# Separate memory for the output projection's split activations, and FNet channel sums over even and odd columns

## The chip, the cores and the metric

One core of a Trainium2 chip runs one layer of a hybrid encoder in float32. The metric is the time of one launch on the device in microseconds, here the median of three runs: 1719.39 (1713.63, 1719.39, 1721.88). The engines are named as in the profile: PE multiplies matrices (PEld are its weight loads), DVE, ACT and POOL do the elementwise work, SP issues most transfers. [...]

## The reference

`x` has 512 positions of 2048 channels. One input projection yields the inputs of four groups of 1024 channels and a gate; each group is normalised, gated, and all are projected back.

```python
h = rms_norm(x, pre_g)
a, f, hy, q, gate = split(h @ w_in)
y_a = silu(layer_norm(depthwise_conv(glu(a)))) @ conv_pw_w + conv_pw_b     # group 0
y_b = fft2(f, axes=(1, 2), norm="ortho").real @ fnet_w + fnet_b            # group 1, FNet
y_c = hyena(hy)                                                            # group 2
y_m = cross_attention(q, mem)                                              # group 3
y = rms_norm_per_group([y_a, y_b, y_c, y_m]) * silu(gate)
return x + rms_norm(y @ w_out, post_g)
```

The change touches three places: the Fourier sums of FNet along its 1024 channels (and the weights after them), the sums of squares of group 0, and the start of the output projection `y @ w_out`.

## The kernel before, in words

All large products are made of three float32r matmuls: each operand is split into a high part (ACT copies it with rounding) and a low part (DVE subtracts), `split`, lines 77 to 83; `mm3` (L111) multiplies high by high, then low by high and high by low in the two cross terms. Since both ACT and DVE make the parts of every weight tile that comes from DRAM (`wload`: a load on SP into one of three `raw` buffers, then `wsplit` into one of three pairs `wh`, `wl`), L79 and L80 are the lines of nearly all their records, and one goes by tiles.

`project` (L313) makes 128 channels of the input projection: two weight tiles of 1024 columns, 24 matmuls of 512 columns under each, so 48 in all. `gate` (L649) is such a projection with a SiLU and a product; `conv_proj` is two of them. `fill` is a generator that is advanced after each 12 matmuls of a projection, so that other work stands between them in the program.

The order of the work: memory keys and values, Hyena filters, Hyena convolutions, FNet (from L661), attention, layer norm and pointwise convolution of group 0 (from L939), the output projection (from L1003). Within this order each engine's own queue is laid out by the framework's planner before the run: at each moment of its estimate an engine takes, of the instructions whose inputs and buffers are there, the one that stands earliest in the program. In the run each engine keeps that order and waits where the estimate was wrong. A tile's buffer is taken from a pool; a tile that comes to lie where a closed pool was waits for that pool's last users.

FNet. The input stage (L678) leaves, for 512 channels, even and odd combinations along the positions in `eeH`/`eeL` (five chunks of 128 channels, the fifth a special row) and `ooH`/`ooL` (four). The channel sums multiply them by cosine and sine tables of 512 columns: three banks `psT` (42 matmuls, one table of 128 x 512 loaded per chunk), a bank `psX` of two-column sums (30 matmuls), two banks `psS` (24 matmuls), lines 728 to 751. After `conv_proj(4)` these banks are split into `teH`, `teL`, `toH`, `toL`, which the sums along the positions read after two more gates (L774). `out_product` (L791) multiplies by `fnet_w` in two halves of four steps, as the filler of `conv_proj(5)` and a gate; in its first step row 0 of `we` is copied by ACT, and one row is loaded into `rx`.

Group 0. With `mean` (L948) DVE subtracts it from eight tiles, ACT squares each and POOL adds the squares to `vacc` (`group_square`, L480); `layer_norm` then sums `vacc` over the channels on PE (L158), ACT and DVE make the reciprocal root, and PE spreads it (L153). It stands in the filler of gate(3, 5), after 36 of its 48 matmuls. The pointwise product's squares are added to `gacc` in the same way (L986). Group 0's last gate follows, then its norm, and 15 DVE operations on its tiles (L500, L998).

The output projection runs in rounds over 512 output columns and in each over 32 pairs of a weight tile and a split activation `jh`, `jl` (L1059); its pool `wp4` is opened where the pool `wp5` of group 0 was closed:

```python
    w5.close()
    w4 = ctx.enter_context(ExitStack())
    wp = w4.enter_context(tc.tile_pool(name="wp4", bufs=3))
    order = [CT * g + ct for g in (2, 1, 3, 0) for ct in range(CT)]
                jh = wt("jh", dt=F32R, bufs=3)
                split(jh[:, c0:c1], jl[:, c0:c1], ys[k // CT][k % CT // 4][:, k % 4, c0:c1])
```

Group 2 comes first in `order`; group 0, the last to be finished, comes last.

Of the kernel before, what the change touches and what calls it, by code (L numbers as in the profile page):

```python
# [20 lines left out]
P = 128  # L21
# [4 lines left out]
KD = D // P  # L26
# [10 lines left out]
C1 = 6.28125  # L37
C2 = 0.0019353071795864769
C3 = 2.0 * math.pi - C1 - float(np.float32(C2))


@with_exitstack
def encoder_kernel(ctx: ExitStack, tc: tile.TileContext, a: dict, out: bass.AP):
# [681 lines left out]
    act.activation(cgxH, cgx[:, 0:10], AF.Copy)  # L725

    NS = ((0, 128), (128, 256), (130, 258))
    psT = [pg() for _ in range(3)]
    psX = pg()
    for c in range(5):  # L730
        raw = load(a["cg"][c], 512)
        th, tl = wsplit(raw[:, 0:512])
        for n in range(3):
            s = slice(*NS[n])
            if c < 4:
                mm3(psT[n], eeH[:, c, s], eeL[:, c, s], th, tl, c == 0, False)
            else:
                pe.matmul(psT[n], eeH[:, c, s], th, start=False, stop=False)
                pe.matmul(psT[n], eeL[:, c, s], th, start=False, stop=True)
    for n in range(3):  # L740
        s = slice(*NS[n])
        for c in range(5):
            pe.matmul(psX[:, 2 * n:2 * n + 2], eeH[:, c, s], cgxH[:, 2 * c:2 * c + 2], start=(c == 0), stop=False)
            pe.matmul(psX[:, 2 * n:2 * n + 2], eeL[:, c, s], cgxH[:, 2 * c:2 * c + 2], start=False, stop=(c == 4))
    psS = [pg() for _ in range(2)]
    for c in range(4):
        raw = load(a["sg"][c], 512)
        th, tl = wsplit(raw[:, 0:512])
        for n in range(2):
            s = slice(P * n, P * n + P)  # L750
            mm3(psS[n], ooH[:, c, s], ooL[:, c, s], th, tl, c == 0, c == 3)
    conv_proj(4, ubm)
    teH = wpo.tile([P, 3, 514], F32R, tag="eeH", name="teH")
    teL = wpo.tile([P, 3, 514], F32R, tag="eeL", name="teL")
    for n in range(3):
        split(teH[:, n, 0:512], teL[:, n, 0:512], psT[n])
        split(teH[:, n, 512:514], teL[:, n, 512:514], psX[:, 2 * n:2 * n + 2])
    toH = wpo.tile([P, 2, 512], F32R, tag="ooH", name="toH")
    toL = wpo.tile([P, 2, 512], F32R, tag="ooL", name="toL")
    for n in range(2):  # L760
# [30 lines left out]
    def out_product():  # L791
        for hf in range(2):
            psE = [pg() for _ in range(4)]
            psO = [pg() for _ in range(2)]
            for k in range(4):
                raw = load(a["fw"][hf, k])
                we, wo = web[:, k % 2, :], wob[:, k % 2, :]
                dve.tensor_tensor(we, raw[:, 512:1024], raw[:, 0:512], op=add)
                dve.tensor_tensor(wo, raw[:, 0:512], raw[:, 512:1024], op=sub)
                if k == 0:  # L800
                    act.activation(we[0:1, :], raw[0:1, 0:512], AF.Copy)
                    rx = stg.tile([P, 1024], F32, tag="raw", name=nm("rx"))
                    dve.memset(rx[:, 0:512], 0.0)
                    sp.dma_start(rx[127:128, 0:512], a["fw"][hf, 0][0:1, 512:1024])
                    xh, xl = wsplit(rx[:, 0:512])
                    for m in range(4):
                        s = slice(P * m, P * m + P)
                        mm3(psE[m][:, 0:258], xh[:, s], xl[:, s], fabH[:, 4, :], fabL[:, 4, :], True, False)
                weH, weL = wsplit(we)
                woH, woL = wsplit(wo)  # L810
                for m in range(4):
                    s = slice(P * m, P * m + P)
                    mm3(psE[m][:, 0:258], weH[:, s], weL[:, s], fabH[:, k, :], fabL[:, k, :], False, k == 3)
                    mm3(psO[m // 2][:, 256 * (m % 2):256 * (m % 2) + 256], woH[:, s], woL[:, s], fobH[:, k, :], fobL[:, k, :], k == 0 and m % 2 == 0, k == 3 and m % 2 == 1)
# [12 lines left out]
            yield  # L827
# [108 lines left out]
    w3.close()  # L936


    w5 = ctx.enter_context(ExitStack())  # L939
    wp = w5.enter_context(tc.tile_pool(name="wp5", bufs=1))  # L940
    lnt = wt("lnt", (P, 4, 512), bufs=1)
    uH = wt("uH", (P, CT, 512), F32R, 1)
    uL = wt("uL", (P, CT, 512), F32R, 1)
    mean = lnt[:, 0, :]
    rstd = lnt[:, 1, :]
    pm = pg()
    pe.matmul(pm, ones, csum, start=True, stop=True)
    act.activation(mean, pm, AF.Copy, scale=1.0 / G)  # L948
# [1 line left out]
    for ct in range(CT):  # L950
        y = acch[ct // 4][:, ct % 4, :]
        dve.tensor_tensor(y, y, mean, op=sub)
        group_square(y, vacc, lnt[:, 2 + ct % 2, :], ct == 0)
    gate(3, 4, yM)

    def layer_norm():
# [16 lines left out]
    for hf in range(2):  # L973
# [8 lines left out]
        for m in range(4):  # L982
            y = yA[hf][:, m, :]
            ct = 4 * hf + m
            act.activation(y, accs[m], AF.Identity, bias=pw_b[:, ct:ct + 1])
            group_square(y, gacc, lnt[:, 2 + ct % 2, :], ct == 0)  # L986
    gA = wt("uL", (P, CT, 512), F32, 1)
    for ct in range(EARLY):
        sp.dma_start(gA[:, ct, :], gdm[:, ct, :])
# [38 lines left out]
    for r, ms in rounds:  # L1028
# [5 lines left out]
        for kp in range(16):  # L1034
# [12 lines left out]
            for kk in range(2):  # L1047
# [8 lines left out]
                    held.append((n, jh, jl, wh, wl))  # L1056
                    continue
                wh, wl = wh2[:, 512 * kk:512 * kk + 512], wl2[:, 512 * kk:512 * kk + 512]
                jh = wt("jh", dt=F32R, bufs=3)  # L1059
                jl = wt("jl", dt=F32R, bufs=3)  # L1060
                split(jh[:, c0:c1], jl[:, c0:c1], ys[k // CT][k % CT // 4][:, k % 4, c0:c1])
                for m in ms:
                    s = slice(P * m, P * m + P)
# [13 lines left out]
def _tables():  # L1077
# [10 lines left out]
    c = np.arange(512)
    ang = 2.0 * np.pi * (np.outer(c, c) % 1024) / 1024.0
    alt = np.tile((-1.0) ** c / P, (P, 1))  # L1090
    t["cg"] = np.concatenate([np.cos(ang).reshape(4, P, 512), alt[None]])
    t["sg"] = np.sin(ang).reshape(4, P, 512)
# [24 lines left out]
def _arrange(inp):  # L1117
# [79 lines left out]
```

## Time and profile before

| | |
|---|---|
| median of three runs | 1719.39 us |
| profiled execution, whole | 1716.29 us |
| its span, first to last instruction | 1714.5 us |
| PE busy | 1655.3 us, 97% of the span |
| DVE busy | 1221.9 us, 71% |
| ACT busy | 813.6 us, 47% |
| POOL busy | 189.9 us, 11% |
| mean granted clock of TensorE | 0.987 |

The page gives shares over the whole span; what a place is worth is read from its own stretch. In a timeline a row is the start, the length, the engine, the line, the operation, what it writes and reads, the shape, and a count; a bracket tells how long the engine had been idle before and whose result ended the wait. Matmuls are pipelined: a row's length is longer than the step to the next row, and it is the step that counts. Steps are taken here between the starts of the first and the last of a number of rows.

### The profile page before, as it was taken

Reading aid. Unit: us, or ns where it says so; the run is one execution under the profiler, and the core shown is the slowest. Engines: PE = TensorE matmul, PEld = TensorE weight load, DVE = VectorE, ACT = ScalarE, POOL = GpSimd, SP = SyncE. Lnnn points to the kernel's source line nnn. Section 1 sums busy time; section 2 is a strip of 40 time slices with the busy share of each in tenths; the row PEclk is TensorE's granted clock in tenths of the full one; section 3 lists DMA queues with packets and bytes.
Section 4 is the critical chain, followed back from the end, with each engine's and each line's share of the span. In section 5 each row is a group of like instructions: output and inputs, shape, how many; then the busy total and the mean of one; then the engine's idle time right before and its main releaser. Section 6 shows DMA issues by size and latency. Waiting matters only on the chain.

```text
span 1714.5 us, 21887 instructions
## 1 busy us (share of the span) xinstructions
PE 1655.3 (97%) x8201; PEld 1386.6 (81%) x8201; DVE 1221.9 (71%) x1835; ACT 813.6 (47%) x1185; POOL 189.9 (11%) x146
## 2 busy tenths in 40 slices
PE   7999999999999999999999999999999699999997
PEld 5997888887777778878888888888878588888876
DVE  7866987378797887989874979985562545454586
ACT  6645655344343443424344355445454434444564
POOL 5101422011020120100000020100212000000000
PEclk9999999999999999999999999999999899999999
DMA  8654545768576684623434334232123523222355
GB/s 290 227 185 156 160 139 158 218 155 176 136 171 150 146 181 126 137 93 106 134 105 133 105 124 153 81 111 86 62 98 109 193 98 102 93 101 98 128 203 179
DMA packets 87487, 240.27 MB, mean 140 GB/s; under 512 B 8915, under 2 KB 26579, under 8 KB 86869
## 3 DMA queue, kind: packets, MB, share of 16 engines
q1 hardware_dynamic: 80468, 213.70, 38.6%
q0 software_dynamic: 6912, 25.17, 7.9%
q8 instruction: 64, 1.05, 0.2%
q14 instruction: 43, 0.34, 0.1%
HBM read 220.21 MB, written 18.63 MB: 139 GB/s over the span
## 4 chain that ended last, share of the span: by engine, by line
PE 78%; DVE 14%; DMA 2%; issue 2%; ACT 2%; POOL 1%; SPq 0%; DVEq 0%; ACTq 0%; POOLq 0%
PE pf L114 14%; PE pf L112 14%; PE pf L113 14%; PE pg L113 11%; PE pg L112 11%; PE pg L114 11%; DVE y L525 5%; DVE wl L80 2%; DVE yc L629 1%; DMA raw<-in_wv_dram 1%; POOL vacc L485 1%; ACT wh L79 1%; DMA wl<-in_w_std_dram 1%; DVE y L630 1%; DVE pq L568 1%
## 5 line engine op out<-in xcount | busy, mean ns | idle before, releaser
L112 PE MATMUL pf<-hH,wh 128*128 128x512 f32 x1280 | 505.6, 395 | 0.0
L114 PE MATMUL pf<-hH,wl 128*128 128x512 f32 x1280 | 502.7, 393 | 0.3 <-DMA wl<-in_w_std_dram 0.3
L113 PE MATMUL pf<-hL,wh 128*128 128x512 f32 x1280 | 502.1, 392 | 0.0
L80 DVE TENSOR_TENSOR wl<-raw,wh 128x1024 fp32r<-128x1024 f32 (+1 forms) x240 | 304.0, 1269 | 151.6 <-ACT wh L79 151.0
L79 ACT ACTIVATE wh<-raw 128x1024 fp32r<-128x1024 f32 (+1 forms) x240 | 247.5, 1033 | 231.3 <-PE pf L113 140.8
L114 PEld LDWEIGHTS pf<-hH,wl 128*128 128x128 f32 x1280 | 241.5, 189 | 49.6 <-DMA wl<-in_w_std_dram 0.7
L113 PEld LDWEIGHTS pf<-hL,wh 128*128 128x128 f32 x1280 | 241.9, 189 | 46.9 <-issue 0.2
L112 PEld LDWEIGHTS pf<-hH,wh 128*128 128x128 f32 x1280 | 241.7, 189 | 46.9 <-issue 0.5
L80 DVE TENSOR_TENSOR jl<-y,jh 128x512 fp32r<-128x512 f32 (+1 forms) x154 | 91.3, 597 | 121.6 <-ACT jh L79 120.5
L79 ACT ACTIVATE jh<-y 128x512 fp32r<-128x512 f32 (+1 forms) x154 | 84.4, 550 | 178.6 <-PE pg L113 113.4
L112 PE MATMUL pg<-wh,jh 128*128 128x512 f32 x384 | 150.6, 392 | 11.2 <-ACT jh L79 11.2
L113 PE MATMUL pg<-wl,jh 128*128 128x512 f32 x384 | 150.5, 392 | 0.0
L114 PE MATMUL pg<-wh,jl 128*128 128x512 f32 x384 | 150.4, 392 | 0.0
L107 ACT ACTIVATE wh<-raw 128x1024 fp32r<-128x1024 f32 x48 | 51.0, 1061 | 99.8 <-PE pf L113 51.8
L525 DVE SCALAR_TENSOR_TENSOR y<-ubuf,par,y 128x512 f32<-128x512 f32 x120 | 93.0, 775 | 3.5 <-ACT y L523 1.5
L112 PEld LDWEIGHTS pg<-wh,jh 128*128 128x128 f32 x384 | 72.8, 189 | 26.6 <-ACT jh L79 11.5
L114 PEld LDWEIGHTS pg<-wh,jl 128*128 128x128 f32 x384 | 72.6, 189 | 15.2 <-DVE jl L80 0.2
L113 PEld LDWEIGHTS pg<-wl,jh 128*128 128x128 f32 x384 | 72.7, 189 | 15.1
L108 POOL DMA_DIRECT2D wl<-in_w_std_dram x48 | 41.7, 870 | 286.2 <-ACT wl L106 274.3
L106 ACT ACTIVATE wl<-raw 128x1024 fp32r<-128x1024 f32 x48 | 50.2, 1046 | 0.0
L525 DVE SCALAR_TENSOR_TENSOR y<-ub,par,y 128x512 f32<-128x512 f32 x60 | 46.4, 773 | 2.3 <-ACT y L523 1.1
L1016 POOL TENSOR_TENSOR xres<-xres,og 128x512 f32<-128x512 f32 x4 | 6.7, 1682 | 372.2 <-ACT og L1015 372.2
(380 smaller groups left out, 2916.8 us busy)
## 6 DMA issues: line engine op xcount, KB each, us to landing
raw<-in_w_std_dram SPq DMA_DIRECT2D x160, 512.0 KB, 4.2
raw<-in_wo_dram SPq DMA_DIRECT2D x77, 512.0 KB, 3.3
wl<-in_w_std_dram POOLq DMA_DIRECT2D x48, 512.0 KB, 7.8
raw<-in_wk_dram SPq DMA_DIRECT2D x16, 512.0 KB, 4.0
kd<-y SPq DMA_DIRECT2D x16, 512.0 KB, 4.9
y<-kd SPq DMA_DIRECT2D x32, 256.0 KB, 6.0
raw<-in_w_f_dram SPq DMA_DIRECT2D x16, 512.0 KB, 3.2
raw<-in_wv_dram SPq DMA_DIRECT2D x15, 512.0 KB, 5.2
```

Source lines behind the costliest of these rows:

```text
L79: act.activation(h, src, AF.Copy)
L80: dve.tensor_tensor(l, src, h, op=sub)
L106: act.activation(l, raw, AF.Copy, scale=-1.0)
L107: act.activation(h, raw, AF.Copy)
L108: pool.dma_start(l, src, accum_op=add)
L112: pe.matmul(ps, wh, xh, start=start, stop=False)
L113: pe.matmul(ps, wh, xl, start=False, stop=False)
L114: pe.matmul(ps, wl, xh, start=False, stop=stop)
L485: pool.tensor_tensor(acc, sqt, acc, op=add)
L525: dve.scalar_tensor_tensor(o, u[:, t:t + L], conv_w[:, ct, t:t + 1], o, op0=mul, op1=add)
L568: dve.tensor_tensor(pq[:, 0], z0, z1, op=add)
L629: dve.scalar_tensor_tensor(yv, pcv[:, h], cinv[:, o, ct:ct + 1], yv, op0=mul, op1=add)
```

## The change

In FNet, the 512 channels and their tables are reordered to even ones first, then odd ones (`FNC`). For half of the output frequencies the even and the odd channels are summed apart, into the two halves of a bank, so each table chunk has 256 columns; `both` then forms even plus odd and even minus odd. The cosine table is loaded as one tile of 1024 columns and one of 256, the sine table as one of 1024. The two-column sums go over three chunks instead of five. The rows of `fnet_w` are ordered to match: row 0 of `we` now comes by a transfer at k = 0, a copy of a row is made at k = 2, and `rx` takes a whole row of 1024 and one more add.

`jh` and `jl` get a pool `wj` of two buffers that is opened before group 0's pool; round 0 uses it alone, later rounds use it for two of three tiles and one buffer in `wp4` for the third. To make room, the four tiles `lnt` become one `stat`; in the layer norm ACT squares into a PSUM bank, and DVE instead of POOL adds the squares, there and after the pointwise product.

```diff
+    cgH, cgL = wload(a["cg"][:, 0:1024])
+    raw = load(a["cg"][:, 1024:1280], 256)
+    caH, caL = wsplit(raw[:, 0:256], 256)
-    for c in range(5):
-        raw = load(a["cg"][c], 512)
-        th, tl = wsplit(raw[:, 0:512])
+    for c in (0, 1, 4, 2, 3):
+        h = c // 2 % 2
+        v = slice(256 * h, 256 * h + 256)
         for n in range(3):
             s = slice(*NS[n])
             if c < 4:
-                mm3(psT[n], eeH[:, c, s], eeL[:, c, s], th, tl, c == 0, False)
+                w_ = slice(256 * c, 256 * c + 256)
+                mm3(psT[n][:, v], eeH[:, c, s], eeL[:, c, s], cgH[:, w_], cgL[:, w_], c % 2 == 0, c == 3)
...
-        for c in range(5):
+        for c in (0, 1, 4):
             pe.matmul(psX[:, 2 * n:2 * n + 2], eeH[:, c, s], cgxH[:, 2 * c:2 * c + 2], start=(c == 0), stop=False)
...
+    sgH, sgL = wload(a["sg"])
-            mm3(psS[n], ooH[:, c, s], ooL[:, c, s], th, tl, c == 0, c == 3)
+            mm3(psS[n][:, v], ooH[:, c, s], ooL[:, c, s], sgH[:, w_], sgL[:, w_], c % 2 == 0, c % 2 == 1)
     conv_proj(4, ubm)
+    def both(ps, odd_first):
+        o_ = wt("odd", (P, 256), bufs=1)
+        act.activation(o_, ps[:, 256:512], AF.Copy)
+        t = wt("bth", bufs=1)
+        dve.tensor_tensor(t[:, 0:256], ps[:, 0:256], o_, op=add)
+        if odd_first:
+            dve.tensor_tensor(t[:, 256:512], o_, ps[:, 0:256], op=sub)
+        else:
+            dve.tensor_tensor(t[:, 256:512], ps[:, 0:256], o_, op=sub)
+        return t
...
-        split(teH[:, n, 0:512], teL[:, n, 0:512], psT[n])
+        split(teH[:, n, 0:512], teL[:, n, 0:512], both(psT[n], False))
...
+                if k == 2:
+                    act.activation(we[0:1, :], raw[0:1, 0:512], AF.Copy)
                 if k == 0:
-                    act.activation(we[0:1, :], raw[0:1, 0:512], AF.Copy)
+                    sp.dma_start(we[0:1, :], a["fw0"][hf:hf + 1, :])
                     rx = stg.tile([P, 1024], F32, tag="raw", name=nm("rx"))
-                    dve.memset(rx[:, 0:512], 0.0)
-                    sp.dma_start(rx[127:128, 0:512], a["fw"][hf, 0][0:1, 512:1024])
+                    dve.memset(rx, 0.0)
+                    sp.dma_start(rx[127:128, :], a["fw"][hf, 0][0:1, :])
+                    dve.tensor_tensor(rx[:, 0:512], rx[:, 0:512], rx[:, 512:1024], op=add)
...
+    wj = ctx.enter_context(tc.tile_pool(name="wj", bufs=2))
     w5 = ctx.enter_context(ExitStack())
...
-    lnt = wt("lnt", (P, 4, 512), bufs=1)
-    mean = lnt[:, 0, :]
-    rstd = lnt[:, 1, :]
+    mean = rstd = wt("stat", bufs=1)
...
-        group_square(y, vacc, lnt[:, 2 + ct % 2, :], ct == 0)
+        sq = vacc if ct == 0 else pg()
+        act.activation(sq, y, AF.Square)
+        if ct:
+            dve.tensor_tensor(vacc, sq, vacc, op=add)
...
-            group_square(y, gacc, lnt[:, 2 + ct % 2, :], ct == 0)
+            sq = gacc if ct == 0 else rstd
+            act.activation(sq, y, AF.Square)
+            if ct:
+                dve.tensor_tensor(gacc, sq, gacc, op=add)
...
-                jh = wt("jh", dt=F32R, bufs=3)
-                jl = wt("jl", dt=F32R, bufs=3)
+                jp, nb = (wj, 2) if r == 0 or n % 3 else (wp, 1)
+                jh, jl = (jp.tile([P, 512], F32R, tag=t, name=nm(t), bufs=nb) for t in ("jh", "jl"))
```

The rest of the diff reorders the tables, `w_f` and `fw` on the host to match.

## Rows read from the trace of the kernel before

**Rows 1.** The page, busy time: us, share of the span, instructions of each engine.

```profile
PE 1655.3 (97%) x8201; PEld 1386.6 (81%) x8201; DVE 1221.9 (71%) x1835; ACT 813.6 (47%) x1185; POOL 189.9 (11%) x146
```

**Rows 2.** PE's waits: total us, times, longest us.

```profile
PE pg L112 <- ACT jh L79: 11.2, 1, 11.2
...
PE pg L113 <- DVE tL L80: 4.9, 6, 1.5
```

**Rows 3.** Timeline, layer norm: DVE, POOL, and PE's sums of `vacc`.

```profile
1235.35 4.30 DVE L952 TENSOR_TENSOR y<-y,lnt 128x512 f32<-128x512 f32 x7
...
1236.84 12.29 POOL L485 TENSOR_TENSOR vacc<-lnt,vacc 128x512 f32<-128x512 f32 x6 [15.70 <-ACT lnt L484]
...
1241.28 2.31 DVE L80 TENSOR_TENSOR wl<-raw,wh 128x1024 fp32r<-128x1024 f32 x1
...
1250.99 1.68 PE L158 MATMUL pg<-ones,vacc 128*128 128x1 f32 x8 [3.50 <-POOL vacc L485]
```

**Rows 4.** Stretches: us, busy of PE, PEld, DVE, ACT, POOL; granted clock, DMA, GB/s.

```profile
913.40:916.60 3.20, 3.20 (x9) 2.48 (x8) 2.22 (x6) 1.59 (x4) 0.00 (x0) 0.50 0.26 93
...
514.20:517.20 3.00, 3.00 (x18) 2.71 (x19) 0.87 (x2) 0.67 (x2) 0.03 (x1) 1.00 0.85 161
...
1251.00:1258.50 7.50, 7.50 (x26) 6.47 (x27) 4.56 (x9) 2.11 (x4) 0.00 (x0) 0.54 0.42 140
...
1352.00:1356.90 4.90, 4.90 (x12) 3.80 (x13) 3.74 (x9) 2.67 (x8) 0.00 (x0) 0.50 0.39 109
```

**Rows 5.** Timeline of PE, FNet channel sums: starts of psT, psX, psS, conv_proj(4).

```profile
899.40 0.59 PE L112 MATMUL pg<-wh,eeH 128*128 128x512 f32 x1
...
909.34 0.17 PE L743 MATMUL pg<-cgxH,eeH 128*128 128x2 f32 x1
...
912.60 0.48 PE L112 MATMUL pg<-wh,ooH 128*128 128x512 f32 x1
...
919.84 0.39 PE L112 MATMUL pf<-hH,wh 128*128 128x512 f32 x1
```

**Rows 6.** Timeline of PE, FNet input stage: 512-column, then 256-column matmuls.

```profile
884.03 0.39 PE L114 MATMUL pf<-hH,wl 128*128 128x512 f32 x1
...
889.02 0.28 PE L112 MATMUL pg<-jh,wh 128*128 128x256 f32 x1
...
890.45 0.28 PE L112 MATMUL pg<-jh,wh 128*128 128x258 f32 x1
```

**Rows 7.** Timeline, first step of `out_product`: ACT's row copy, PE's first use.

```profile
972.78 0.63 ACT L801 ACTIVATE web<-raw 1x512 f32<-1x512 f32 x1 [0.59 <-DVE web L798]
...
975.80 0.28 PE L112 MATMUL pg<-faH,wh 128*128 128x258 f32 x1
```

**Rows 8.** Groups by form, 896 to 920: busy us, mean ns, idle before.

```profile
L80 DVE TENSOR_TENSOR teL<-pg,teH 128x512 fp32r<-128x512 f32 x3 | 2.0, 685 | 2.4 <-ACT teH L79 2.4
...
L80 DVE TENSOR_TENSOR ooL<-pg,ooH 128x256 fp32r<-128x256 f32 x4 | 1.6, 421 | 0.2
```

**Rows 9.** DMA issues: count, KB each, median us from issue to landing.

```profile
dec<-in_decay_dram SPq DMA_DIRECT2D x1, 16.0 KB, 4.0
```

**Rows 10.** Timeline, start of the output projection: PE, DVE, ACT.

```profile
1335.14 0.95 PE L158 MATMUL pg<-ones,gaccA 128*128 128x1 f32 x8
...
1341.32 2.08 DVE L500 SCALAR_TENSOR_TENSOR y<-y,par,rsg 128x512 f32<-128x512 f32 x3 [1.48 <-ACT rsg L154]
...
1351.16 1.67 ACT L79 ACTIVATE jh<-y 128x512 fp32r<-128x512 f32 x3 [9.88 <-DVE y L998]
...
1351.85 0.80 PE L112 MATMUL pg<-wh,jh 128*128 128x512 f32 x1 [11.19 <-ACT jh L79]
```

**Rows 11.** Timeline, round 0 of the output projection: ACT and DVE after a release.

```profile
1365.26 0.63 ACT L79 ACTIVATE jh<-y 128x512 fp32r<-128x512 f32 x1 [2.09 <-PE pg L113]
...
1365.92 0.69 DVE L80 TENSOR_TENSOR jl<-y,jh 128x512 fp32r<-128x512 f32 x1 [2.03 <-ACT jh L79]
...
1366.87 1.23 DVE L80 TENSOR_TENSOR wl<-raw,wh 128x1024 fp32r<-128x1024 f32 x1 [0.26 <-ACT wh L79]
```

More of the change, by code (lines that the diff above doesn't have):

```diff
@@ L39 @@
 C3 = 2.0 * math.pi - C1 - float(np.float32(C2))
+FNC = np.concatenate([np.arange(0, 512, 2), np.arange(1, 512, 2)])
 @with_exitstack
@@ L735, in encoder_kernel @@
             if c < 4:
-                mm3(psT[n], eeH[:, c, s], eeL[:, c, s], th, tl, c == 0, False)
-            else:
-                pe.matmul(psT[n], eeH[:, c, s], th, start=False, stop=False)
-                pe.matmul(psT[n], eeL[:, c, s], th, start=False, stop=True)
+                w_ = slice(256 * c, 256 * c + 256)
+                mm3(psT[n][:, v], eeH[:, c, s], eeL[:, c, s], cgH[:, w_], cgL[:, w_], c % 2 == 0, c == 3)
+            else:
+                pe.matmul(psT[n][:, v], eeH[:, c, s], caH, start=False, stop=False)
+                pe.matmul(psT[n][:, v], eeL[:, c, s], caH, start=False, stop=True)
     for n in range(3):
         s = slice(*NS[n])
-        for c in range(5):
+        for c in (0, 1, 4):
             pe.matmul(psX[:, 2 * n:2 * n + 2], eeH[:, c, s], cgxH[:, 2 * c:2 * c + 2], start=(c == 0), stop=False)
@@ L745, in encoder_kernel @@
     psS = [pg() for _ in range(2)]
+    sgH, sgL = wload(a["sg"])
     for c in range(4):
-        raw = load(a["sg"][c], 512)
-        th, tl = wsplit(raw[:, 0:512])
+        v = slice(256 * (c // 2), 256 * (c // 2) + 256)
+        w_ = slice(256 * c, 256 * c + 256)
         for n in range(2):
             s = slice(P * n, P * n + P)
-            mm3(psS[n], ooH[:, c, s], ooL[:, c, s], th, tl, c == 0, c == 3)
+            mm3(psS[n][:, v], ooH[:, c, s], ooL[:, c, s], sgH[:, w_], sgL[:, w_], c % 2 == 0, c % 2 == 1)
     conv_proj(4, ubm)
+    def both(ps, odd_first):
[8 more added lines that the diff above has]
+        return t
     teH = wpo.tile([P, 3, 514], F32R, tag="eeH", name="teH")
@@ L760, in encoder_kernel @@
     for n in range(2):
-        split(toH[:, n, :], toL[:, n, :], psS[n])
+        split(toH[:, n, :], toL[:, n, :], both(psS[n], True))
     gate(2, 6, yC)
@@ L1087, in _tables @@
     t["etab"] = e.reshape(4, 2, P, 256).transpose(2, 0, 1, 3).reshape(P, 2048)
[L1088 to L1092, printed above, removed]
+    ang = 2.0 * np.pi * (np.outer(FNC, i) % 1024) / 1024.0
+    alt = np.tile((-1.0) ** i / P, (P, 1))
+    t["cg"] = np.concatenate([np.cos(ang).reshape(4, P, 256).transpose(1, 0, 2).reshape(P, 1024), alt], axis=1)
+    sin = np.sin(ang)
+    sin[256:, 0] = (-1.0) ** i
+    t["sg"] = sin.reshape(4, P, 256).transpose(1, 0, 2).reshape(P, 1024)
     cgx = np.zeros((P, 5, 2))
@@ L1141, in _arrange @@
     wf = w[:, 2 * G:3 * G]
-    r["w_f"] = np.concatenate([wf[:, :512], wf[:, mir]], axis=1).reshape(KD, P, 1024)
+    r["w_f"] = np.concatenate([wf[:, FNC], wf[:, mir[FNC]]], axis=1).reshape(KD, P, 1024)
     par["conv_w"] = v["conv_dw_w"][0].T.reshape(CT, P, W31).transpose(1, 0, 2)
@@ L1149, in _arrange @@
     fw = v["fnet_w"][0]
-    r["fw"] = np.stack([fw[:512], fw[mir]]).reshape(2, 4, P, 2, 512).transpose(3, 1, 2, 0, 4).reshape(2, 4, P, 1024)
+    j = np.arange(1, 256)
+    k0 = np.concatenate([[256], j, [512], 512 - j])
+    k1 = np.concatenate([[768], 1024 - j, [512], 512 + j])
+    r["fw0"] = fw[0].reshape(2, 512)
+    r["fw"] = np.stack([fw[k0], fw[k1]]).reshape(2, 4, P, 2, 512).transpose(3, 1, 2, 0, 4).reshape(2, 4, P, 1024)
     par["fn_b"] = cm(v["fnet_b"][0])
```

## The prediction

> **What bounds the kernel now.** I read the page's busy line first: PE is busy 97% of the span [rows 1], so a change pays where it takes columns from PE, closes a hole in PE, or lifts PE's clock after a hole. The waits of PE come next: one wait of 11.2 us stands far above the rest [rows 2], and a search of PE's timeline for holes finds only one more that this change touches, of 3.50 us before the sums of `vacc` [rows 3]. [...] Then the timelines of the three places.
>
> **FNet channel sums: fewer columns.** Today the stretch from the first `psT` matmul to the first of `conv_proj(4)` lasts 899.40 to 919.84 = 20.44 us [rows 5]: 42 matmuls of 512 columns (9.94 us), 30 of two columns (3.26 us, 0.109 each), 24 of 512 (7.24 us). After it: 42 of 256, 18 of two, 24 of 256. What 256 columns cost is seen in the input stage just before: 22 matmuls of 512 columns take 884.03 to 889.02, 0.227 each; 12 of 256 take 889.02 to 890.45, 0.119 each [rows 6]. So 42 x 0.119 + 18 x 0.109 + 24 x 0.119 = 9.8 us, **10.6 saved**. That takes the clock as 1.00 throughout. Today it falls after 30 two-column matmuls [rows 4]; with 18, over 2.0 us, it may not. If it falls for as long as now (3.3 us at half clock, where 512 columns take some 0.41, 12 of them in 4.9 us [rows 4], and 256 so about 0.21), 1.5 us are lost again: 9.1 saved is the lower end. I take 10.6, since the input stage holds 1.00 on 256 columns.
>
> [...]
>
> Around it: the tables come in three loads and splits instead of nine. The first split is 1024 wide, but its slot is split while PE still runs the input stage, as two 512-wide ones are now. The fifth chunk is now third in order, about 2.1 us after the start, and needs `eeL` of chunk 4, which today comes about then: **0.3 lost**, bounds 0 to 0.8.
>
> `both` adds, for each of five banks, an ACT copy of 256 columns (no dearer than the 512-wide copies of 0.63 [rows 7]) and two DVE operations of 256 (0.42 by the nearest row [rows 8]). ACT and DVE hand over to each other, about 2.7 us a bank, 13 us in all. I cost it at nothing: `teH` is next read by PE after `conv_proj(4)` and two gates, 144 matmuls of 0.227 = 33 us. Without that cover it would cost its 13 us. ACT's and DVE's queues behind it hold the weight splits of `conv_proj(4)`, one of each per 24 matmuls (5.4 us); the chain leaves about half of each engine free.
>
> **`out_product`.** The ACT copy of row 0 (0.63, ends 973.41) becomes a DMA on SP that waits for DVE's `we`; behind it on SP are only weight loads that already wait for buffers. PE wants the split of `we` at 975.80 [rows 7]. The only small load with a landing time took 4.0 us [rows 9]: 972.78 + 4.0, then ACT 0.63 and DVE 0.69, gives 978.1, 2.3 late; a landing near 2 us would be barely late. Twelve ready matmuls of the projection beside it (2.7 us) can go in between. **0.5 lost**, bounds 0 to 2.5. The wider `rx` memset, its DVE add and the copy at k = 2 lie early enough in both halves.
>
> **Start of the output projection.** PE's last sums before it end at 1336.09; then ACT's `jh` waits for DVE's last L998, since `jh` lies in memory of the layer-norm pool, and PE starts at 1351.85 [rows 10]. With its own memory `jh`, `jl` for n = 0 and 1 are split long before (their source, `yC`, is finished, and ACT and DVE have idle time). PE then runs 24 matmuls at once, 5.45 us, with the eight L153 matmuls among them, to about 1342.7. n = 2 finds its buffer free when n = 0 ends, about 1338.8, and its `jl` fits on DVE before 1341.32. For n = 3 DVE is in its 15 scaling operations, which are earlier in the program and all ready, until 1351.1 [rows 10]: its `jl` comes behind them. Eight of its twelve matmuls need no `jl`. So 24 + 12 + 8 = 44 matmuls, 44 x 0.227 = 10.0 us, move ahead of the moment at which PE starts today; what is late next is `jl` of n = 3, a hole of about 4.4 us, longer than the 3.50 that halved the clock, so the slow stretch after it stays. L153 now stands behind matmuls: 0.5 off. **9.5 saved**. Bounds: 32 matmuls if `jl` of n = 2 also falls behind the scaling, 7.3; all of 15.8 less about 1.5 for L153, and the slow stretch too (4.9 us at 0.50 [rows 4], 2.4 us), 16.7.
>
> **Layer norm.** PE waits 3.50 us for the last of POOL's seven adds, six of which fill 1236.84 to 1249.13 [rows 3], then runs 1251.0 to 1258.5 at 0.54 [rows 4], which loses 7.5 x 0.46 = 3.4 us. Hole and clock: 6.9 us. After the change ACT squares into PSUM and DVE adds. No row shows ACT writing PSUM; 512 columns from SBUF to SBUF take it 0.63 [rows 11], a PSUM operand moves DVE's time from 0.61 [rows 3] to 0.69 [rows 8], so 0.55 to 0.71 on ACT, I take 0.63; it is not the pace. DVE is: from 1235.35 seven subtractions (4.30, [rows 3]) and seven adds with a PSUM operand (0.69 each, [rows 8]) reach 1244.5, three microseconds ahead of the 1247.49 at which PE asks. But the weight split that DVE did at 1241.28 is later in the program and goes behind the adds and one gate's pair of operations, to about 1246.4; PE reaches its third matmul on those weights 11 matmuls before 1247.49, at about 1245.2. A new wait of 1.2 us, too short, by the 1.5 us hole, to cost clock: **5.7 saved**, bounds 0 and 6.9. In the pointwise stage the adds move likewise, hidden by a 48-matmul gate.
>
> **Sum.** 10.6 + 9.5 + 5.7 - 0.3 - 0.5 = 25.0 us. The profiled execution took 1716.29 (span 1714.5), so 1691.3; it lies 3.1 under the median of the three runs, 1719.39, and on that footing the forecast is **1694**.
>
> **Rivals.** The hole before the output projection closes wholly, because `jl` of n = 3 slips in: 1687. For it: DVE idles just before 1341; against it: the scaling operations are always ready. Or the hole stays, because the planner leaves DVE's first `jl` behind the scaling and only ACT's part moves: 1703; DVE idles before 1341.32 [rows 10], which speaks against it. Or the adds on DVE delay the weight split by as much as POOL delayed the sums, so that nothing is gained there: 1700. Both of these, with the small losses at their ends: 1703 + 5.7 + 2.5 = 1711. Or the weight load under each matmul sets the pace in this stage, so that 256 columns save a quarter of the 0.227 and not half: 66 x 0.05 = 3.3 less, 1697; two columns under the same loads take 0.109 [rows 5], which all but excludes it. [...]
>
> On the slower side: round 0 has two buffers of `jh` and `jl` where there were three. From release of a buffer to `jl` takes 1365.26 to 1366.61 = 1.35 us now; with a weight split queued ahead (1.23 on DVE, about as much on ACT) some 3.6 [rows 11]. PE gives it the 12 matmuls of one n, 2.72. Past that point each of 16 pairs stalls 0.9 us, 14 us, and if such holes kept the clock at 0.50 for the round, 384 x 0.2 = 77 more: 1785. Against it: today `jl` goes ahead of the weight split, and a hole of 1.5 us left the clock at 1.00. [...]
>
> **Chances.** Forecast 0.58, wholly closed 0.12, hole stays 0.12, adds delay 0.08, columns no cheaper 0.02, both fail 0.04, two buffers 0.04. The range takes the bounds: gains at most 10.6 + 16.7 + 6.9 = 34.2 (1685 on the median's footing), at least 9.1 + 7.3 + 0 - 3.3 = 13.1 (1706); with a microsecond for the runs, 1684 to 1707. Half a per cent, 8.6 us, is about what a measurement of this kernel tells from no change: faster 0.92, same 0.04, slower 0.04.
>
> **What would show it.** After: the FNet stretch at about 10 us with granted clock 1.00; the first `jh` split well before the last gate ends; PE's largest wait at 4 to 5 us, for `jl`; no POOL adds in the layer norm and no hole before its sums, but a short one for `wl`. Wrong if `wl` or `wh` waits appear around `conv_proj(4)`, if `we` stalls PE by more than its filler, or if round 0 shows a wait for `jh` at each n.

## The result, and the profile after

The changed kernel takes 1692.44 us (median of four runs, 1689.61 to 1693.59), beside 1718.13 of the kernel before (four runs, 1713.63 to 1721.88): a ratio of 0.985, 95% interval 0.982 to 0.988, so 25.7 us. The profiled execution took 1689.61 us with a span of 1687.8, 26.7 less than the span before. The forecast was 1694, from 25.0 us.

First the page's busy line, to be read beside [rows 1]:

```profile
PE 1640.4 (97%) x8189; PEld 1374.3 (81%) x8189; DVE 1226.5 (73%) x1855; ACT 812.5 (48%) x1184; POOL 172.1 (10%) x132
```

Then the list of PE's waits (engine, line that waits, whom it waits for, total us, times, longest), beside [rows 2]:

```profile
PE pg L116 <- ACT wh L83: 10.3, 4, 6.2
PE pg L117 <- DVE tL L84: 4.7, 6, 1.3
...
PE pg L157 <- DVE diag L156: 3.0, 2, 2.7
...
PE pg L118 <- DVE jl L84: 1.9, 1, 1.9
```

The 11.2 us for `jh` are gone, and so are the 3.50 for POOL's `vacc`. In the change's own places three waits are left: 2.7 us for the spread of the last norm, which the kernel before had too, ahead of its 11.2; 1.9 for a `jl`; and 0.31 for `cgxH`, in the timeline below. PE's busy time fell by 14.9 only: the rest of the 26.7 is idle time.

Five sums over the channels cut every trace into the same stretches. Their rows after (count, ns of one, first and last start):

```profile
L162 PE MATMUL pg<-ones,gaccB x8: 169/250/250, 1020.4 to 1021.1; 128*128 128x1 f32 x8
L162 PE MATMUL pg<-ones,gaccM x8: 169/250/250, 1215.2 to 1215.9; 128*128 128x1 f32 x8
L162 PE MATMUL pg<-ones,vacc x8: 169/250/250, 1235.2 to 1235.9; 128*128 128x1 f32 x8
L162 PE MATMUL pg<-ones,gaccA x8: 169/250/250, 1317.7 to 1318.4; 128*128 128x1 f32 x8
```

The table, in us, has the differences of such first starts, for the two kernels and the main experiments below; "FNet input" is the one matmul on `acc5`, just before the channel sums.

| stretch | before | after | fnet_only | fnet_ln | no_fnet | norm_pf | norm_pf_late | all_holes |
|---|---|---|---|---|---|---|---|---|
| start to FNet input | 899.2 | 898.1 | 899.6 | 902.5 | 898.8 | 897.9 | 901.8 | 897.9 |
| FNet, to sums of gaccB | 132.0 | 122.3 | 122.0 | 125.8 | 133.7 | 122.2 | 121.8 | 121.6 |
| attention, to gaccM | 194.4 | 194.8 | 195.3 | 195.4 | 194.6 | 195.4 | 194.8 | 195.4 |
| to sums of vacc | 25.4 | 20.0 | 25.4 | 19.9 | 19.9 | 20.0 | 19.9 | 20.0 |
| to sums of gaccA | 84.1 | 82.5 | 84.2 | 82.6 | 82.5 | 82.5 | 82.6 | 82.6 |
| output projection | 379.4 | 370.1 | 380.2 | 380.1 | 370.1 | 370.2 | 363.4 | 362.4 |

So the change gave 9.7 in FNet, lost 0.4 in attention, gave 5.4 + 1.6 = 7.0 around the layer norm and 9.3 in the output projection: 25.6. The other 1.1 lie in the first row, where none of these kernels differs from the others but all_holes, which loads a small table there: that row alone runs from 897.9 to 902.5, so single spans say little and stretches say much.

**FNet.** PE's timeline after, as [rows 5]: starts of `psT`, `psX`, `psS` and of `conv_proj(4)`:

```profile
898.31 0.47 PE L116 MATMUL pg<-wh,eeH 128*128 128x256 f32 x1
...
901.47 0.27 PE L752 MATMUL pg<-cgxH,eeH 128*128 128x2 f32 x1 [0.31 <-ACT cgxH L729]
...
906.00 0.37 PE L116 MATMUL pg<-wh,ooH 128*128 128x256 f32 x1
...
908.91 0.40 PE L116 MATMUL pf<-hH,wh 128*128 128x512 f32 x1
```

Two stretches of it: us, busy of PE, PEld, DVE, ACT, POOL, then the granted clock (as a share of the full one), DMA share and GB/s:

```profile
906.00:908.90 2.90, 2.90 (x26) 2.90 (x26) 2.63 (x6) 1.14 (x4) 0.00 (x0) 1.00 0.64 213
908.90:914.90 6.00, 6.00 (x29) 4.96 (x28) 3.89 (x8) 3.36 (x7) 0.00 (x0) 1.00 0.48 163
```

898.31 to 908.91 is 10.60 where it was 20.44. The clock stays at 1.00 in both. The two-column matmuls now begin after 21 others, and there PE waits for `cgxH`, the small table they read.

**Layer norm.** Timeline of DVE and PE around the sums of `vacc`, as [rows 3]:

```profile
1234.00 0.68 DVE L984 TENSOR_TENSOR vacc<-pg,vacc 128x512 f32<-128x512 f32 x1
1234.60 1.21 DVE L84 TENSOR_TENSOR wl<-raw,wh 128x1024 fp32r<-128x1024 f32 x1
...
1234.93 0.40 PE L117 MATMUL pf<-hL,wh 128*128 128x512 f32 x1
1235.16 0.95 PE L162 MATMUL pg<-ones,vacc 128*128 128x1 f32 x8
1235.97 0.48 PE L118 MATMUL pf<-hH,wl 128*128 128x512 f32 x1
```

And the stretch around them:

```profile
1235.00:1238.00 3.00, 3.00 (x19) 2.63 (x18) 3.00 (x5) 1.83 (x3) 0.00 (x0) 1.00 0.31 100
```

No hole, clock 1.00. The last add ends at 1234.68, the sums start at 1235.16, and the first matmul on the late `wl` follows at 1235.97, 0.16 after that `wl` is done (1234.60 + 1.21 = 1235.81).

**Start of the output projection**, timeline as [rows 10]:

```profile
1317.71 0.95 PE L162 MATMUL pg<-ones,gaccA 128*128 128x1 f32 x8
1321.38 1.22 PE L157 MATMUL pg<-diag,ones 128*128 128x128 f32 x4 [2.72 <-DVE diag L156]
1322.26 0.77 PE L116 MATMUL pg<-wh,jh 128*128 128x512 f32 x1
...
1324.55 2.08 DVE L504 SCALAR_TENSOR_TENSOR y<-y,par,rsg 128x512 f32<-128x512 f32 x3 [1.62 <-ACT rsg L158]
...
1327.57 0.63 ACT L83 ACTIVATE jh<-y 128x512 fp32r<-128x512 f32 x1 [3.05 <-PE pg L117]
...
1333.47 0.68 DVE L84 TENSOR_TENSOR jl<-y,jh 128x512 fp32r<-128x512 f32 x1
...
1334.21 1.19 PE L118 MATMUL pg<-wh,jl 128*128 128x512 f32 x4 [1.90 <-DVE jl L84]
```

The stretches behind the two holes:

```profile
1321.40:1326.40 5.00, 5.00 (x16) 4.38 (x17) 2.54 (x6) 0.60 (x1) 0.00 (x0) 0.50 0.99 367
1334.20:1338.00 3.80, 3.79 (x17) 3.14 (x18) 3.65 (x6) 3.08 (x9) 0.00 (x0) 1.00 0.45 128
```

The kernel before had the first of these waits too:

```profile
1338.81 0.71 PE L153 MATMUL pg<-diag,ones 128*128 128x128 f32 x4 [2.72 <-DVE diag L152]
```

PE still idles 2.72 us behind the sums and then runs 5 us at half clock. It gives back the buffer of n = 0 so late that `jh` of n = 2 is made at 1327.57; DVE is in the scalings from 1324.55 on, and the `jl` of n = 2 comes at 1333.47. So 32 matmuls, not 44, stand ahead of 1334.21; the hole there is 1.90, and the clock behind it is 1.00.

**What was to be hidden.** `both` starts on ACT at 904.11 and its last split, on DVE, ends at 919.52; PE reads `teH` at 952.46, with no idle before it. The transfer of row 0 of `we` goes out at 961.65, and ACT goes on with that tile 1.5 us later:

```profile
904.11 0.39 ACT L767 ACTIVATE odd<-pg 128x256 f32<-128x256 f32 x1 [0.32 <-PE pg L118]
...
918.83 0.69 DVE L84 TENSOR_TENSOR toL<-bth,toH 128x512 fp32r<-128x512 f32 x1 [0.70 <-ACT toH L83]
...
952.46 0.28 PE L116 MATMUL pg<-clH,teH 128*128 128x258 f32 x1
...
961.65 0.25 SPq L827 DMA_DIRECT2D web<-in_fw_dram  x1
...
963.16 0.63 ACT L83 ACTIVATE wh<-web 128x512 fp32r<-128x512 f32 x1 [1.89 <-DVE wob L822]
```

### The profile page after: what moved, and what is told of

Its sections match the earlier page's. It is cut to its first block, busy times and chain, and to the rows that moved or that the text cites. A ratio compares the mean times of both kernels' runs of the same rounds, so it can differ in the third digit from the quotient of the medians.

```text
span 1687.8 us, 21827 instructions
## 1 busy us (share of the span) xinstructions
PE 1640.4 (97%) x8189; PEld 1374.3 (81%) x8189; DVE 1226.5 (73%) x1855; ACT 812.5 (48%) x1184; POOL 172.1 (10%) x132
## 4 chain that ended last, share of the span: by engine, by line
PE 79%; DVE 14%; issue 2%; ACT 2%; DMA 2%; SPq 0%; POOL 0%; DVEq 0%; ACTq 0%; POOLq 0%
PE pf L118 15%; PE pf L117 15%; PE pf L116 15%; PE pg L117 11%; PE pg L116 11%; PE pg L118 11%; DVE y L529 5%; DVE wl L84 2%; DVE yc L633 1%; DMA raw<-in_wv_dram 1%; ACT wh L83 1%; DVE y L634 1%; DVE pq L572 1%; DMA kdm<-mst 0%; PE pg L628 0%
## 5 line engine op out<-in xcount | busy, mean ns | idle before, releaser
L84 DVE TENSOR_TENSOR wl<-raw,wh 128x1024 fp32r<-128x1024 f32 (+2 forms) x234 | 293.3, 1256 | 116.3 <-ACT wh L83 115.8
L83 ACT ACTIVATE wh<-raw 128x1024 fp32r<-128x1024 f32 (+2 forms) x234 | 244.4, 1045 | 209.0 <-PE pf L117 124.0
```

What stands on the lines that cost most here:

```text
L83: act.activation(h, src, AF.Copy)
L84: dve.tensor_tensor(l, src, h, op=sub)
```

## The experiments

### One part alone, and one part left out

fnet_only has the FNet part alone; fnet_ln adds the layer norm; no_fnet is the kernel before with all but FNet. The memory alone was not run; the change makes room for it where the four `lnt` tiles were. Against the changed kernel, fnet_ln is:

```diff
-    wj = ctx.enter_context(tc.tile_pool(name="wj", bufs=2))
...
-                jp, nb = (wj, 2) if r == 0 or n % 3 else (wp, 1)
-                jh, jl = (jp.tile([P, 512], F32R, tag=t, name=nm(t), bufs=nb) for t in ("jh", "jl"))
+                jh = wt("jh", dt=F32R, bufs=3)
+                jl = wt("jl", dt=F32R, bufs=3)
```

> FNet's part of the change alone; the layer norm and the memory of jh and jl are as in the kernel before. Theory (three independent gains): FNet alone gives 9.8 on its channel sums and 1.1 on their earlier start, of which some 10.4 last, so 1718.1 - 10.4 = 1707.7; the hole of 3.5 us before the sums of vacc and the 11.2 us wait for jh stand as before. Rival (the gain is given back at a later wait that does not move): the hole before the output projection grows by what FNet saved, and the time stays at 1716 to 1718.

> FNet and the layer norm (one stat tile, squares into PSUM, adds on DVE), but jh and jl in wp4 with three buffers as before. Theory: the layer norm is worth hole and clock, 6.9 to 7.0, so 1707.7 - 7 = 1700.7, with no PE hole before the sums of vacc and the 11 us wait for jh still there. Rival as in the prediction: a wait for wl takes 1.2 of it, 1702; or the adds on DVE delay wl by all of it, 1707.7.

> The layer norm and the memory of jh and jl alone; FNet as in the kernel before. Theory (independent gains): 7.0 for the layer norm and 9.3 to 10 for the start of the output projection, so 1715.5 - 16.7 = 1698.8, and the FNet stretch from the first psT to the first of the next projection lasts 20.4 with the slow clock behind its 30 two-column matmuls. Rival (one of the two gains needs the shorter FNet, or part of it was only where the run began): 1703 or above.

Measured: fnet_only 1708.44 beside 1716.09 (ratio 0.995, interval 0.994 to 0.997), fnet_ln 1702.61 (0.992, 0.991 to 0.994), no_fnet 1700.33 beside 1717.30 (0.991, 0.989 to 0.993). The columns of the table say it more sharply: each stretch has its gain as soon as its own part is in, and no other. The 5.4 + 1.6 of the layer norm appear with the layer norm, with or without FNet (25.4 to 19.9 or 20.0); the output projection takes 380 without the memory and 370.1 with it, with or without FNet. By these stretches the gains are independent and nothing is given back later. fnet_ln's median lies nearer to the rival's 1702 than to the theory's 1700.7, but its two stretches around the layer norm, 19.9 and 82.6, are those of the changed kernel, so no wait for `wl` took a part of them. fnet_only's median lies 7.7 under its kernel before (interval 5.5 to 10.1), not 10.4: of the 10.0 that its FNet stretch gained, 0.9 and 0.8 are missing in the attention and output stretches and 0.4 in the first row, where its code is that of before. Whether these are chance stays open.

One number of no_fnet misses what was expected. With the code of before, its FNet stretch takes 133.7 where that of before takes 132.0, and from the first `psT` matmul to the first of `conv_proj(4)` it lasts 899.09 to 921.08 = 21.99 us, where 20.4 were expected: its clock falls 2.7 us into the run of two-column matmuls, is 0.50 from 912.40 to 917.00 and low until about 918.5. And where the changed kernel runs at half clock behind the 2.72 us, no_fnet, with the same wait, doesn't:

```profile
1333.22 0.71 PE L153 MATMUL pg<-diag,ones 128*128 128x128 f32 x4 [2.72 <-DVE diag L152]
...
1333.20:1338.20 5.00, 4.98 (x25) 4.14 (x26) 3.40 (x8) 1.23 (x2) 0.00 (x0) 1.00 0.99 413
```

It then waits 3.3 for the `jl` of n = 2, and its output projection takes the same 370.1. So the length of a hole alone does not settle the clock behind it.

fnet_ln's profile, of the slowest of its six executions (1708.03; the others took 1699.58 to 1704.15), brought something unforeseen. Its FNet stretch is 3.5 longer than that of the changed kernel, with the same code up to there:

```profile
907.93 0.27 PE L752 MATMUL pg<-cgxH,eeH 128*128 128x2 f32 x1 [2.31 <-ACT cgxH L729]
```

The stretch behind that hole:

```profile
907.90:913.90 6.00, 5.97 (x39) 5.97 (x39) 2.41 (x4) 2.75 (x4) 0.00 (x0) 0.72 0.18 67
```

And the DMA issue of the table (count, KB, us from issue to landing):

```profile
cgx<-in_cgx_dram SPq DMA_DIRECT2D x1, 5.0 KB, 4.4
```

The wait for `cgxH` is 2.31, the clock behind it 0.72, and the load of 5 KB took 4.4 us from issue to landing; the same row of the changed kernel has 2.4, that of fnet_only 2.2, that of norm_pf_late 1.7.

### The small table loaded early

```diff
+    cgx = cst.tile([P, 16], F32, tag="cgx", name="cgx")
+    sp.dma_start(cgx[:, 0:10], a["cgx"])
+    cgxH = cst.tile([P, 10], F32R, tag="cgxH", name="cgxH")
+    act.activation(cgxH, cgx[:, 0:10], AF.Copy)
     yB = [ytile(4), ytile(5)]
...
-    cgx = wt("cgx", (P, 16), F32, 1)
-    sp.dma_start(cgx[:, 0:10], a["cgx"])
...
```

> The whole change, with the small table of the two-column sums in memory of its own and loaded before the input stage of FNet. Theory: the new FNet stretch now asks for that table 3 us after its start instead of 10 us, and its load, which starts only 0.4 us after that start because it waits for memory of the closed pool, lands 2.5 to 4.5 us later; so the hole ahead of the two-column matmuls (0.3 in the profile of the changed kernel, 2.3 with a slow clock behind it in that of FNet and layer norm) is gone, the stretch from the first psT to the first of the next projection is 10.0 to 10.3, and the median is 0.3 to 3 below the changed kernel's 1692.4. Rival (the fifth chunk's eeL is what PE waits for there, and the load only lies beside it): a hole of 0.3 to 0.5 stays, now for eeL, and nothing is gained.

Measured: no PE wait is left in the stretch, and it lasts 901.66 to 911.73 = 10.07 us; 1690.84 beside 1714.43 (ratio 0.985, 0.983 to 0.987), which the times alone don't tell from the changed kernel. The profiles whose FNet code is otherwise that of the change order themselves by this wait: no wait, 9.97 (one_buf, below) and 10.07 (cgx_early, norm_pf_late, all_holes); 0.21, 10.48 (norm_pf); 0.31, 10.60; 2.31, 14.03 (fnet_ln). fnet_only has 10.35 with no idle listed, though there too the first two-column matmul starts 0.06 behind ACT's copy of the table, as in the changed kernel. The rival, a wait for `eeL` in its place, did not come: the planner put five two-column matmuls into that gap, and they are what met the late table.

### The bank of the last norm

In the built program the spread (L157) stands directly behind the column sums, ahead of every matmul of round 0, though `jh`, `jl` and the weights of n = 0 are ready. The edit takes the norm's two banks from the other pool:

```diff
-    group_norm(0, gacc, yA)
+    group_norm(0, gacc, yA, pf)
```

With it the planner puts 15 matmuls of round 0 between the sums and the first spread. So a bank of that pool was what held them; that it was one of the norm's own, wanted by an accumulator of round 0, is inferred from this.

> The whole change, with the two banks of the last norm taken from the projection's pool (pf) instead of pg. Theory: the 2.72 us idle of PE before the spread stands because the first accumulator of the output projection comes to lie in the bank of the norm's column sums; with another bank 15 matmuls go ahead of the first spread and the 2.72 are filled. But jl of n = 3 still comes behind the 15 scalings, at about 1334, so what is filled comes back as a longer wait for jl: 5 us where it is 1.9, and the time is within 2 of the changed kernel's 1692.4. Rival (the start alone limits): all of 2.72 and the slow clock behind it are saved, 1687.5.

Measured: 1690.19 (1689.65 to 1690.40) beside 1716.09 (ratio 0.985, 0.983 to 0.986), 2.2 under the changed kernel's median where the theory allowed 2; the stretches below bear the theory out. The 2.72 are filled. PE frees the first buffer earlier, `jl` of n = 2 is made at 1322.26, ahead of the scalings, and 44 matmuls run before PE waits for the `jl` of n = 3, now for 4.42 us and with the slow clock behind it:

```profile
1322.26 0.69 DVE L84 TENSOR_TENSOR jl<-y,jh 128x512 fp32r<-128x512 f32 x1 [0.45 <-ACT jh L83]
...
1334.37 2.08 PE L118 MATMUL pg<-wh,jl 128*128 128x512 f32 x4 [4.42 <-DVE jl L84]
```

The stretch behind it:

```profile
1334.40:1339.40 5.00, 5.00 (x12) 3.98 (x13) 5.00 (x8) 3.96 (x9) 0.00 (x0) 0.50 0.59 155
```

The output projection takes 370.2 where it took 370.1: one idle of 4.42 stands for two of 2.72 and 1.90, and 5 us at half clock, 2.5 lost, stand behind the one as they stood behind the first of the two. The twelve more matmuls ahead of the wait, 2.7 us, came back as a longer wait, since DVE's scalings end when they did.

### The scalings between the pairs

```diff
-    group_norm(0, gacc, yA)
...
-    for ct in range(EARLY):
-        group_scale(0, ct, yA)
...
+    channel_rstd(rsg[0], gacc, pf)
+    def scaling():
+        group_scale(0, EARLY, yA)
+        for ct in range(EARLY):
+            yield
+            group_scale(0, ct, yA)
...
+            elif r == 0 and 2 <= kp < 10:
+                next(scale0, None)
```

The closing of group 0's pool and the opening of `wp4` move with the scalings, to kp = 10 of round 0.

> As norm_pf, and the 15 scalings of group 0 stand in the program between the pairs of round 0 (two for each of the kp from 2 on) instead of ahead of round 0. Theory: both holes (2.72 and 1.9) close, and with them the slow clock from 1321.4 to 1326.5, about 2.2 us: 1692.4 - 6.8 = 1685.6, and no PE wait above 1 us between the column sums and the end of round 0. Rival (DVE has no room for scalings beside the splits): waits for jl or wl of a microsecond or more appear in round 0 and the time stays at 1690 or above.

> The whole change, with all three remaining holes closed: the last norm in the other banks, the scalings between the pairs of round 0, the small table loaded early. Theory: the gains add up, 1683.5 - 0.3 to 3 = 1681 to 1683, and PE has no wait above 1 us from the start of the FNet channel sums to the end of round 0 except those that stood in the kernel before. Rival: the table's wait had been covered, 1683.5 as without it.

Measured: norm_pf_late 1683.49 beside 1716.09 (ratio 0.981, 0.980 to 0.983); all_holes, with the early table too, 1682.77 (1681.64 to 1685.12) beside 1714.43 (0.981, 0.979 to 0.983). Both beat the changed kernel: their medians lie 9 to 10 us lower, and the gains over the kernel before, each measured with its own, are 6 to 7 larger (32.6 and 31.7 beside 25.7). The table's part is too small for the times to show. In all_holes PE does not stop in either place (stretches of FNet and of round 0):

```profile
898.00:910.00 12.00, 12.00 (x95) 11.65 (x94) 8.31 (x17) 7.46 (x15) 0.00 (x0) 1.00 0.62 206
1317.00:1400.00 83.00, 83.00 (x375) 68.98 (x375) 51.45 (x72) 37.59 (x55) 0.00 (x0) 1.00 0.42 154
```

The output projection goes from 370.1 to 363.4 and 362.4: 6.7 and 7.7, where 2.72 + 1.90 idle and 2.2 of slow clock were foreseen. Both runs also have the norm's other banks; the scalings moved alone were not run.

### One buffer instead of two

The prediction's slower rival was a stall at each n of round 0. No such wait appears with two buffers; this run makes it happen.

```diff
-    wj = ctx.enter_context(tc.tile_pool(name="wj", bufs=2))
+    wj = ctx.enter_context(tc.tile_pool(name="wj", bufs=1))
...
-                jp, nb = (wj, 2) if r == 0 or n % 3 else (wp, 1)
+                jp, nb = (wj, 1) if r == 0 or n % 3 == 0 else (wp, 2)
```

> The whole change, with one buffer of jh and jl in round 0 instead of two (three in the later rounds, as before). It measures what the slower rival of the prediction would cost: PE waits at each of the 31 later n for its jh and jl. Theory (short holes leave the clock alone): a turnaround of 0.7 to 1.4 at each n, 22 to 43 us, granted clock 1.00 through the round, in all 1714 to 1736. Rival (repeated short holes hold the clock at 0.50): 77 us more, about 1790 to 1810, with a granted clock near 0.50 to 0.60 in round 0.

Measured, one run: 1715.17, with 399.2 for the output projection instead of 370.1. PE's wait in the list:

```profile
PE pg L116 <- ACT jh L83: 16.3, 31, 1.4
```

Two of its stalls in the timeline:

```profile
1354.37 0.50 PE L116 MATMUL pg<-wh,jh 128*128 128x512 f32 x1 [0.49 <-ACT jh L83]
...
1357.88 0.50 PE L116 MATMUL pg<-wh,jh 128*128 128x512 f32 x1 [0.49 <-ACT jh L83]
```

And a stretch of round 0:

```profile
1345.00:1400.00 55.00, 47.11 (x190) 33.88 (x188) 20.25 (x24) 17.67 (x24) 0.00 (x0) 1.00 0.21 69
```

The step from stall to stall is 3.51 us where 12 matmuls take 2.72, so 0.79 each, 31 x 0.79 = 24 of the 29. Most of the rest lies at the start: the wait for the first late `jl` is 3.63 where it was 1.90, with 0.68 over the 5 us behind it. Over the 55 us of stalls the clock is 1.00: short holes at this spacing did not lower it in this run.

### The cover of `both` taken away

```diff
+    conv_proj(4, ubm)
+    gate(2, 6, yC)
+    gate(2, 7, yC)
     psT = [pg() for _ in range(3)]
...
-    conv_proj(4, ubm)
...
-    gate(2, 6, yC)
-    gate(2, 7, yC)
```

> The whole change, with conv_proj(4) and the two gates of group 2 moved ahead of the channel sums, so that nothing stands between the sums and their next readers: the cover of the five both chains is taken away. Theory: the chain is in all 13 to 15 us, and of it three banks' part lies behind the last psT matmul, 3 us of it beside psS: PE idles 5 to 6 us before the first te matmul, 3 to 5 more for to, and the clock falls to 0.50 for some 5 us, 2.5 lost: 11 to 13 above the changed kernel, 1703 to 1705. Rival (ACT and DVE pipeline the five banks, so little shows): under 5.

Measured, one run: 1691.94, against the theory. PE's timeline where the wait should have been:

```profile
952.99 0.28 PE L118 MATMUL pg<-clH,teL 128*128 128x258 f32 x1
953.11 0.39 PE L116 MATMUL pf<-hH,wh 128*128 128x512 f32 x1
...
953.57 0.28 PE L116 MATMUL pg<-clH,teH 128*128 128x258 f32 x1
...
967.12 0.74 PE L116 MATMUL pg<-faH,wh 128*128 128x258 f32 x4 [0.47 <-ACT faH L83]
...
969.45 0.39 PE L116 MATMUL pg<-faH,wh 128*128 128x258 f32 x1 [0.47 <-ACT wh L83]
```

The planner took matmuls of the next projection, `conv_proj(5)`, and laid them between the `te` products as each bank came. A little was lost behind them: two waits of 0.47 that the changed kernel does not have, and the stretch from FNet's input to the sums of `gaccB` takes 123.8 where it took 122.3. The rival (under 5) holds, though for another reason than it gave: the cover moved in from behind.

### A longer run of two-column matmuls

```diff
+    for i in range(24):
+        j = 16 + 2 * (i // 6)
+        pe.matmul(psX[:, j:j + 2], eeH[:, i % 3, 0:128], cgxH[:, 0:2], start=(i % 6 == 0), stop=(i % 6 == 5))
     conv_proj(4, ubm)
```

> The whole change with 24 more two-column matmuls, whose result nobody reads, in one run behind the sine sums. It asks what made the clock fall in the kernel before, where 30 of them stood in one run. Theory (the run of narrow matmuls itself, while PE is busy throughout): with 24 in a row the clock falls to 0.50 for about 3 us, and 24 x 0.11 = 2.6 us plus 1.5 to 2 of slow clock are added. Rival (13 in a row left it at 1.00 and 24 do too; what fell before fell for another reason): 2.6 are added and the granted clock stays 1.00.

Measured, one run of 1694.03: 24 in a row from 909.37 to 911.97, 2.60 us, and the clock stays at 1.00 behind them. The stretch there:

```profile
912.00:918.00 6.00, 6.00 (x28) 4.94 (x29) 3.03 (x9) 2.32 (x7) 0.00 (x0) 1.00 0.29 91
```

The same place in no_fnet, with the 30 of the kernel before:

```profile
912.40:917.00 4.60, 4.60 (x13) 3.73 (x13) 2.02 (x5) 2.33 (x6) 0.00 (x0) 0.50 0.33 104
```

The theory falls for 24. 13 and 24 in a row left the clock at 1.00; with 30, half clock came in both traces that have them: behind the run in [rows 4], and in no_fnet from its 26th matmul on, where the step goes from 0.11 to 0.21. So 24 may be just too few. Whether it is the run's length or what stands around it (256-column matmuls before the 24, 512-column ones before the 30) is open.

## Why the prediction was right, point by point

**FNet, 10.6 less 0.3.** The mechanism and the price of the columns held: without the wait the stretch lasts 10.07, and the prediction had 9.8 + 0.3 = 10.1. Of the 10.6, 1.8 (7.24 - 24 x 0.227) is not columns but clock, lost behind the 30 two-column matmuls of the kernel before; no_fnet, with the same code, lost 1.5 more, so this part differs between profiles. What it missed is that the order changed around the small table. Before, `psX` came 10 us after the start; now the fifth chunk waits for `eeL`, the planner fills that gap with `psX`, and the load of `cgx`, issued 0.4 us after the start because it lies in memory of a closed pool, has 3 us to land instead of 10. The term is 0 to 0.5 in all profiles but one, and 4.0 in that (14.03 against 10.07). The clock did not fall behind 13 two-column matmuls (1.00 from 906.00 to 914.90), so the lower end of 9.1 did not come from there. The rival in which 256 columns save a quarter of the 0.227 is out: it would give 66 x 0.17 + 2.0 = 13.2.

The same 5 KB took 1.7, 2.2, 2.4 and 4.4 us from issue to landing in four profiles, so one measured landing is a poor bound for a load that PE waits for.

**`both`, cost nothing.** Right, and the chain took 15.4 us beside the splits where 13 were foreseen. The sentence that it would cost its 13 us without cover was not borne out: both_bare took the named cover away and its stretch grew by 1.5, since the following projection has matmuls that are ready.

**`out_product`, 0.5 less.** ACT goes on with the row's tile 1.5 us after the load goes out, so the load had landed by then (bound 4.0), and PE has no wait there; the term was nothing.

**Layer norm, 5.7.** It gave 7.0, hole and clock, where 6.9 were named. The step that failed is the new wait of 1.2 for `wl`. The late split came as foreseen, but PE took the two matmuls that need only `wh`, and then the planner put the sums of `vacc`, 0.8 us long, into the place where PE would have waited. They come earlier in the queue than the prediction held fixed. And that split took 1.21 us, where the one beside POOL's adds had taken 2.31 [rows 3]. All six kernels of the table with the new layer norm repeat the 19.9 to 20.0. That a wait of 1.2 would be too short to cost clock rested on one hole, of 1.46 us, that ends at 514.20 and has 1.00 behind it [rows 4]; the kernel before itself has a wait of 1.65, ending at 786.04, with 0.66 over the 5 us behind it, so that ground was too thin.

**Start of the output projection, 9.5.** It gave 9.3, by other terms than those of the sum. The step that failed is that PE runs matmuls as soon as its sums are done: a bank was held by the norm, by what norm_pf shows. PE idled 2.72, freed the buffer of n = 0 after DVE had begun the scalings, and so the `jl` of n = 2 too fell behind them: 32 matmuls, 32 x 0.227 = 7.3, the lower bound of the text. But the second hole was then 1.90 instead of 4.4, and the clock behind it stayed at 1.00, which gives back the 2.4 that the text left lost (the slow stretch moved forward, into time that was idle before). 7.3 + 2.4 = 9.7, beside 9.3 measured. norm_pf freed the bank and gave the picture of the prediction in each step (44 matmuls, `jl` of n = 2 ahead of the scalings, one hole of 4.42, half clock behind it), with 379.4 - 370.2 = 9.2. So the step was wrong, its price was right, and the sum agreed because two errors cancelled. The clock's share is luck in part: in cgx_early the wait at the same place is 2.47, with 0.69 over the 4 us behind it, and the output projection takes 371.2.

**Rivals.** "Wholly closed" was priced at 7 us under the forecast; norm_pf_late, with the norm's banks and the scalings moved, shows that price (6.7 in the stretch). The slower rival's stall did not come with two buffers. With one, PE loses 0.79 at each n, near the 0.9 a pair that the rival used, and the clock stays at 1.00, which speaks against its 77 us of half clock: without them it would have been some 14 us, not 91.

## What to carry to other kernels

Filling a hole pays only if no later one grows, so follow the chain to its next stop: here letting PE start earlier gave nothing by itself, and what paid was that together with moving the fifteen operations ahead of one `jl` on DVE. A planner that fills gaps turns a wait you price into another instruction's early start, so look at what that instruction reads and when it was loaded, and at which PSUM bank its result goes to. Compare traces by stretches between marks that both have: here the stretch to the first mark ran from 895.5 to 902.5 us over the twelve profiles, and the others, for the same code, mostly differed by 1 or less. And do not credit the clock behind a hole from one profile: the same hole of 2.72 us was followed by 1.00 in no_fnet and by 0.50 in the changed kernel.

## What was not expected of the hardware

- Idle of PE and the clock behind it: the length of the idle alone did not settle it. 1.90 us in the changed kernel and 2.12 in both_bare left it at 1.00, while 2.31 in fnet_ln had 0.72 over the 6 us behind it and 2.47 in cgx_early 0.69 over 4 us; but the 2.72 ahead of the last spread had 0.50 in the changed kernel and 1.00 in no_fnet, and an idle of 1.65 in the kernel before had 0.66 where 1.48, at 185.02, left 1.00. In norm_pf_late 1.98 was followed by 0.50:

```profile
185.45 0.77 PE L424 MATMUL pg<-fwH,h2s 128*128 128x512 f32 x1 [1.98 <-DVE y L460]
...
185.40:190.40 5.00, 4.95 (x12) 3.96 (x13) 5.00 (x11) 2.64 (x5) 0.47 (x2) 0.50 0.88 259
```

  In fnet_ln, too, this hole is 2.0; it and norm_pf_late have the longest first stretches of the table (902.5 and 901.8). In the two kernels, fnet_only and norm_pf it is 1.5. In one_buf 31 stalls of about half a microsecond, one every 3.5 us, left the clock at 1.00.
- With a run of 30 two-column matmuls, PE busy throughout, half clock came twice: 0.50 from 913.40, behind the run, in the kernel before, and from 912.40, within it, in no_fnet. Behind runs of 13 (changed kernel) and 24 (two_col_24) it was 1.00.
- The 5 KB load from DRAM on SP's queue took from 1.7 us (norm_pf_late) to 4.4 us (fnet_ln) in the same place of the program.
